# Moving the second low part of each weight load from VectorE to GpSimd

## The chip, the cores and the metric

The kernel runs on one core of a Trainium2 chip. The metric is device time in microseconds (us). A core has five engines that run side by side, each working through its own queue in order and waiting on semaphores: TensorE (PE in the profile; PEld are its weight loads), VectorE (DVE), ScalarE (ACT), GpSimd (POOL) and SyncE (SP), which here issues nearly all DMA transfers. VectorE, ScalarE and GpSimd work on SBUF, the on-chip memory of 128 partitions; TensorE writes its products to PSUM, from where VectorE or ScalarE take them.

## The reference

One layer of a hybrid network runs over 384 tokens: 128 of a context stream and 256 of a latent stream, with a model width of 2048.

```python
z = h @ w_in                                  # h: normalised, modulated input
zs = _token_shift(z[..., :N_SHIFTED], mu_prev, mu_next)
r, k, v, wd, ad = ...                         # slices of zs
w_lin = w0 + einsum(tanh(wd), w2);  a = sigmoid(a0 + einsum(ad, a2))
sa = S @ a_t                                  # scan, both directions, 32 heads of 64 x 64
S = S * w_t + outer(sa, b_t) + outer(v_t, k_t);  y = S @ r_t
y_a = (groupnorm(y) + bonus) * silu(g_a) @ w_out_a
y_b = (b_gate * conv3(c_gate * x_b) * silu(g_b)) @ w_out_b
merged = sigmoid(m_a) * y_a + sigmoid(m_b) * y_b
out = x + gate * (merged @ w_o)
```

All inputs are float32. The large matrices (w_in with 20,864 columns, w_out_a, w_out_b, w_o) make up most of the work.

## The kernel before, in words

A float32 product is made of three products of a rounded format: each operand x is split into a high part (a cast) and a low part (x minus the high part), and TensorE adds high x high, high x low and low x high (`mm3`, lines 80 to 83). For a weight, ScalarE casts the high part (`whi`, line 88) and VectorE subtracts to get the low part (`wlo`, line 89); both happen in `split`.

Dense work is a stream of column pairs (`Stream`). A pair is two blocks of 128 columns over 2048 rows, loaded in two halves of 1024 rows. A half is one call of `wload`: it takes a buffer `raw` (two in rotation, 1 MB each, filled by one DMA or by two when the columns are apart), and splits it in two parts of 512 rows, q = 0 and q = 1. `whi` and `wlo` each have three buffers. TensorE uses a part in 24 matmuls. There are 95 pairs: `rk` (r and k of a head pair), `gv` (gate and v), `ma`, `mb`, `bc`, `bx`, `bg`, `gb` (gates and convolution), `ob` and `oa` (the output projections of the branches). A `raw` buffer is free for its next load when both subtractions from it are done.

The recurrence runs in 16 blocks b of two heads. Block b goes through `prep_a` and `prep_k` (decays and keys), `prep_b` (triangular systems), `prep_c` (transposes) and `scan` (two chains of chunks in both directions), then `norm` and `finish`. The steps on which this document rests are these.

- `prep_b` multiplies `pr` and `bk` on TensorE (`pA`, line 703), VectorE masks the result into `A` (line 709), and the diagonal blocks go through DRAM into a tile `U` of 48 partitions: `ui<-A` (line 713) and `U<-ui` (line 719), both on SP. VectorE then runs sixty dependent operations on `U` and `ut` (lines 724 and 726), after which SP writes `uo<-U` (line 729) and reads it back, `A<-uo` (line 734). VectorE transposes two pieces (`x<-A`, line 737), which TensorE needs at the scan's start (`pH`, line 842).
- Meanwhile GpSimd scales `bk` (line 716), and the next block's `prep_a` multiplies low-rank weights (`pl`, line 627 through `mm3`), whose low part `lwl` VectorE makes in `split` too, and a sum of squares (`pn`) whose low part is `lo_sq` (line 605). v is shifted on VectorE (lines 422 and 424).
- In `scan`, TensorE's `pu` goes to the state `st` on VectorE (L831 at the first step, L833 later), the state to `po` on TensorE (line 804), that to `sav` on VectorE (L805), and so on. The next block's `prep_k` (L646, L647, L654, L659 to L661) shares VectorE's queue with it.
- GpSimd also clears a part of `A` (line 863) and takes a power in `norm` (line 929).

TensorE's queue is written out by hand: the generators yield numbers of dense steps to put between their own matmuls. The queues of the other engines are set by the framework's scheduler, from its own estimates and priorities, and it is run anew for every version of the program.

Of the kernel before, what the change touches and what calls it, by code (L numbers as in the profile page):

```python
# [9 lines left out]
F32 = mybir.dt.float32  # L10
F32R = mybir.dt.float32r
AF = mybir.ActivationFunctionType
ALU = mybir.AluOpType
AX = mybir.AxisListType

P = 128
# [40 lines left out]
def hybrid_step(ctx, tc, cst, x_prompt, x_sample, state_f, state_b, c, c_ctx, ada_w, ada_b, norm_g,  # L57
# [3 lines left out]
    V, S, G, TE = nc.vector, nc.scalar, nc.gpsimd, nc.tensor  # L61
# [6 lines left out]
    wp = ctx.enter_context(tc.tile_pool(name="wp", bufs=3))  # L68
# [13 lines left out]
        TE.matmul(out, wh, xl, start=False, stop=False)  # L82
        TE.matmul(out, wl, xh, start=False, stop=stop)  # L83

    def split(src, shape, th, tl, pool, nm, rows=P):
        hi = pool.tile(shape, F32R, tag=th, name=f"{th}_{nm}")
        lo = pool.tile(shape, F32R, tag=tl, name=f"{tl}_{nm}")
        S.copy(hi[0:rows], src)  # L88
        V.tensor_tensor(lo[0:rows], src, hi[0:rows].bitcast(F32), ALU.subtract)  # L89
        return hi, lo  # L90


# [3 lines left out]
    def wload(view, k0, cols, nm):  # L96

        w = P * len(cols)
        raw = wp.tile([P, 8, w], F32, tag="raw", name=f"raw_{nm}", bufs=2)
        if cols[-1] == cols[0] + P:  # L100
            nc.sync.dma_start(raw[:], view[:, k0:k0 + 8, cols[0]:cols[0] + 256])
        else:
            for i, c0 in enumerate(cols):
                nc.sync.dma_start(raw[:, :, i * P:(i + 1) * P], view[:, k0:k0 + 8, c0:c0 + P])
        res = [split(raw[:, 4 * q:4 * q + 4, :], [P, 4, w], "whi", "wlo", wp, f"{nm}_{q}") for q in range(2)]
        return res


# [2 lines left out]
    class Stream:  # L111
# [14 lines left out]
        def load(self, j):  # L126
            p, half = divmod(j, 2)
            self.extend(p)
            if j not in self.ready and p < len(self.pairs):
                tag, view, cols = self.pairs[p][:3]  # L130
                self.ready[j] = wload(view, 8 * half, cols, f"{tag}_{half}")
# [207 lines left out]
    def early_load(g):  # L339
        raw = wp.tile([P, 2, EW], F32, tag="raw", name=f"eraw_{g}", bufs=2)  # L340
        o = 0
        for c0, w in ecols:
            nc.sync.dma_start(raw[:, :, o:o + w], win[:, 2 * g:2 * g + 2, c0:c0 + w])
            o += w
        return split(raw[:], [P, 2, EW], f"ehi{g % 2}", f"elo{g % 2}", pp, f"{g}")
# [212 lines left out]
    for m in range(4):  # L558
# [10 lines left out]
        src = t[0:96, ::-1] if m % 2 else t[0:96, :]  # L569
# [38 lines left out]
    def prep_a(b, o):  # L608
# [9 lines left out]
        for m in range(4):  # L618
            if m % 2 == 0:
                lraw = sp.tile([96, 2, P], F32, tag="lraw", name=f"lraw_{b}_{m}")  # L620
                nc.sync.dma_start(lraw[:], (w2, a2)[m // 2][0][:, :, bs].rearrange("d r n -> r d n"))
                with tc.issue_after(box["kn"]) if m == 0 and "kn" in box else ExitStack():
                    lwh, lwl = split(lraw[:], [96, 2, P], "lwh", "lwl", sp, f"{b}_{m}", rows=96)
                yield 2
            pl = bank(f"pl_{b}_{m}")
            pl = flat(pl[:, 0:3, :])
            mm3(pl, lwh[:, m % 2, :], lwl[:, m % 2, :], l_hi[:, m, :], l_lo[:, m, :], True, True)
            t = tmp(f"sig_{b}_{m}")
            S.activation(t[:], pl, AF.Sigmoid, bias=pcol((W0, W0 + 16, A0, A0 + 16)[m] + b))
            sig.append(t)  # L630
            yield 2
# [329 lines left out]
    for b in range(NB):  # L961
# [17 lines left out]
        w = WINDOW + (FIRST if b == 0 else LAST if b == NB - 1 else 0)  # L979
# [108 lines left out]
    for nq in range(3):  # L1088
# [8 lines left out]
        for q in range(4):  # L1097
            raw = wp.tile([P, 4, 512], F32, tag="raw", name=f"raw_wo{nq}_{q}", bufs=2)
            nc.sync.dma_start(raw[:], wov[:, 4 * q:4 * q + 4, ns])
            for e in range(2):  # L1100
                hi, lo = split(raw[:, 2 * e:2 * e + 2, :], [P, 2, 512], "whi", "wlo", wp, f"wo{nq}_{q}_{e}")
# [11 lines left out]
    for half in range(2):  # L1113
        c0 = 1536 + 256 * half
        wt = []
        for q2 in range(2):
            raw = wp.tile([P, 8, 256], F32, tag="raw", name=f"raw_wl{half}_{q2}", bufs=2)
# [4 lines left out]
        for s in range(3):  # L1122
# [5 lines left out]
            for k in range(KC):  # L1128
                hi, lo = wt[k // 4]
# [3 lines left out]
            if half == 1:  # L1133
                f = rsf[:, s, :]
# [37 lines left out]
```

## Time and profile before

| | |
|---|---|
| runs of the kernel before | 2236.75, 2238.54, 2238.73 us, median 2238.54 |
| profiled execution | 2234.36 us, span 2232.6 us, granted TensorE clock 0.998 |
| TensorE, matmuls | 2173.1 us busy, 97% of the span |
| VectorE | 1553.3 us busy, 70% |
| ScalarE | 1013.5 us busy, 45% |
| GpSimd | 115.7 us busy, 5% |
| HBM | 305.80 MB read, 26.21 MB written |

A row of a timeline has start, duration, engine, line, operation, tile written and tiles read, shapes and count; in brackets the idle time before it and what ended it. Merged rows (x2, x3) give the time from the first start to the last end. "PEq" or "SPq" marks an engine's sequencer; a DMA's issue is shown there, not its transfer. A row of waits has the total in us, the number of times, and the longest. A row of a group has its busy time, the mean of one in ns, and the idle time before.

### The profile page before, as it was taken

The numbers are of one execution on the slowest core, as the hardware profiler recorded it, in microseconds if no ns is written. First come the engines' busy times: TensorE is split into PE (matmuls) and PEld (weight loads), VectorE is DVE, ScalarE is ACT, GpSimd is POOL, SyncE is SP. The second block draws the span as 40 slices with busy tenths as digits, with TensorE's granted clock in tenths as the row PEclk, the third lists the DMA queues.
The fourth block names the chain that finished last, engine by engine and source line by source line (L and its number), as shares of the span: only waits on it lengthen the run. The fifth ranks groups of instructions, "written<-read, shape, count | busy, mean of one in ns | idle before, by whom it ended". The sixth has DMA issues, their size and how long they took to land.

```text
span 2232.6 us, 40518 instructions
## 1 busy us (share of the span) xinstructions
PE 2173.1 (97%) x16020; PEld 2062.7 (92%) x16020; DVE 1553.3 (70%) x3240; ACT 1013.5 (45%) x1784; POOL 115.7 (5%) x113
## 2 busy tenths in 40 slices
PE   5999999999999999999999999999999999999998
PEld 3589999999999999999999999999999999998988
DVE  3259567787878878777878787887777785444354
ACT  4245435454545454444445454546454633333333
POOL 2000000000000000000000000000000000000000
PEclk9999999999999999999999999999999999999999
DMA  9974454444343435343444434344445464886633
GB/s 338 346 211 128 131 141 116 116 117 118 108 132 107 130 100 131 106 130 100 121 108 127 112 107 133 107 122 126 124 118 139 144 196 143 294 281 233 220 132 113
DMA packets 426574, 335.25 MB, mean 150 GB/s; under 512 B 82496, under 2 KB 408720, under 8 KB 425488
## 3 DMA queue, kind: packets, MB, share of 16 engines
q1 hardware_dynamic: 424896, 330.91, 50.2%
q8 instruction: 126, 2.06, 0.4%
q10 hardware_dynamic: 432, 1.57, 0.2%
q14 instruction: 64, 0.52, 0.1%
q0 software_dynamic: 1056, 0.19, 0.1%
HBM read 305.80 MB, written 26.21 MB: 149 GB/s over the span
## 4 chain that ended last, share of the span: by engine, by line
PE 74%; DVE 12%; DMA 6%; ACT 4%; issue 2%; SPq 1%; POOL 0%; POOLq 0%; DVEq 0%; ACTq 0%
DMA raw_adah<-in_ada_w_dram 4%; PE d_rk L81 3%; PE d_rk L82 3%; PE d_rk L83 3%; PE d_gv L81 3%; PE d_gv L82 3%; PE d_gv L83 3%; PE d_oa L81 2%; PE pA L703 2%; PE d_oa L83 2%; PE d_oa L82 2%; PE d_mb L81 2%; PE d_mb L83 2%; PE d_mb L82 2%; PE d_bc L81 2%
## 5 line engine op out<-in xcount | busy, mean ns | idle before, releaser
L724 DVE TENSOR_TENSOR ut<-U 48x30 f32<-48x30 f32 (+14 forms) x480 | 154.8, 323 | 18.3 <-DMA U<-ui 5.5
L81 PE MATMUL d_rk<-h_hi,whi_rk 128*128 128x384 f32 x480 | 161.7, 337 | 0.6 <-ACT lst L554 0.6
L726 DVE TENSOR_TENSOR U<-U,ut 48x30 f32<-48x30 f32 (+14 forms) x480 | 154.5, 322 | 11.1
L81 PE MATMUL d_gv<-h_hi,whi_gv 128*128 128x384 f32 x480 | 160.6, 335 | 0.0
L82 PE MATMUL d_rk<-h_lo,whi_rk 128*128 128x384 f32 x480 | 160.5, 334 | 0.0
L83 PE MATMUL d_rk<-h_hi,wlo_rk 128*128 128x384 f32 x480 | 160.4, 334 | 0.0
L83 PE MATMUL d_gv<-h_hi,wlo_gv 128*128 128x384 f32 x480 | 160.4, 334 | 0.0
L82 PE MATMUL d_gv<-h_lo,whi_gv 128*128 128x384 f32 x480 | 160.4, 334 | 0.0
L88 ACT CAST whi_gv<-raw_gv 128x1024 fp32r<-128x1024 f32 (+1 forms) x64 | 64.0, 999 | 139.6 <-PE d_rk L82 100.0
L88 ACT CAST whi_rk<-raw_rk 128x1024 fp32r<-128x1024 f32 x60 | 63.0, 1054 | 110.8 <-PE d_rk L82 34.7
L89 DVE TENSOR_TENSOR wlo_rk<-raw_rk,whi_rk 128x1024 fp32r<-128x1024 f32 x60 | 72.9, 1218 | 45.3 <-ACT whi_rk L88 35.6
L81 PE MATMUL d_bc<-h_hi,whi_bc 128*128 128x384 f32 x256 | 92.2, 360 | 0.0
L81 PE MATMUL d_gb<-h_hi,whi_gb 128*128 128x384 f32 x256 | 92.2, 360 | 0.0
L81 PE MATMUL d_bg<-h_hi,whi_bg 128*128 128x384 f32 x256 | 92.2, 360 | 0.0
L81 PE MATMUL d_bx<-h_hi,whi_bx 128*128 128x384 f32 x256 | 92.1, 360 | 0.0
L81 PE MATMUL d_ma<-h_hi,whi_ma 128*128 128x384 f32 x256 | 91.6, 358 | 0.0
L81 PEld LDWEIGHTS d_rk<-h_hi,whi_rk 128*128 128x128 f32 x480 | 90.1, 188 | 0.9 <-ACT lst L554 0.9
L81 PE MATMUL d_mb<-h_hi,whi_mb 128*128 128x384 f32 x256 | 90.4, 353 | 0.0
L81 PEld LDWEIGHTS d_gv<-h_hi,whi_gv 128*128 128x128 f32 x480 | 90.1, 188 | 0.2
L81 PE MATMUL d_ob<-ybh,whi_ob 128*128 128x384 f32 x256 | 88.4, 345 | 2.0 <-DVE smb L521 1.0
L82 PEld LDWEIGHTS d_rk<-h_lo,whi_rk 128*128 128x128 f32 x480 | 90.2, 188 | 0.0
L82 PEld LDWEIGHTS d_gv<-h_lo,whi_gv 128*128 128x128 f32 x480 | 90.1, 188 | 0.0
(315 smaller groups left out, 6548.4 us busy)
## 6 DMA issues: line engine op xcount, KB each, us to landing
raw_adah<-in_ada_w_dram SPq DMA_DIRECT2D x64, 512.0 KB, 8.7
raw_rk<-in_w_in_dram SPq DMA_DIRECT2D x60, 512.0 KB, 5.3
raw_gv<-in_w_in_dram SPq DMA_DIRECT2D x60, 512.0 KB, 4.9
raw_ma<-in_w_in_dram SPq DMA_DIRECT2D x16, 1024.0 KB, 5.6
raw_mb<-in_w_in_dram SPq DMA_DIRECT2D x16, 1024.0 KB, 5.6
raw_bc<-in_w_in_dram SPq DMA_DIRECT2D x16, 1024.0 KB, 5.5
raw_bx<-in_w_in_dram SPq DMA_DIRECT2D x16, 1024.0 KB, 5.4
raw_bg<-in_w_in_dram SPq DMA_DIRECT2D x16, 1024.0 KB, 5.5
```

The lines of the kernel that those rows point to most:

```text
L81: TE.matmul(out, wh, xh, start=start, stop=False)
L82: TE.matmul(out, wh, xl, start=False, stop=False)
L83: TE.matmul(out, wl, xh, start=False, stop=stop)
L88: S.copy(hi[0:rows], src)
L89: V.tensor_tensor(lo[0:rows], src, hi[0:rows].bitcast(F32), ALU.subtract)
L703: TE.matmul(pas[h, n // 4 * 4][:, n % 4, :], bk[hss[h], n, :], pr[hss[h], n, :], start=True, stop=True)
L724: V.tensor_tensor(tv, U[:, 0:s, s:s + 1].broadcast_to([48, s, w]), U[:, s:s + 1, s + 1:].broadcast_to([48, s, w]), ALU.mult)
L726: V.tensor_tensor(U[:, 0:s, s + 1:], U[:, 0:s, s + 1:], tv, ALU.add)
```

## The change

The helper `split` gets a parameter for the engine that subtracts, and `wload` passes VectorE for the first part of a half and GpSimd for the second. All other users of `split` keep VectorE. The file becomes one line longer, so from there on the lines of the changed kernel are one higher.

```diff
-    def split(src, shape, th, tl, pool, nm, rows=P):
+    def split(src, shape, th, tl, pool, nm, rows=P, eng=V):
         hi = pool.tile(shape, F32R, tag=th, name=f"{th}_{nm}")
         lo = pool.tile(shape, F32R, tag=tl, name=f"{tl}_{nm}")
         S.copy(hi[0:rows], src)
-        V.tensor_tensor(lo[0:rows], src, hi[0:rows].bitcast(F32), ALU.subtract)
+        eng.tensor_tensor(lo[0:rows], src, hi[0:rows].bitcast(F32), ALU.subtract)
         return hi, lo
...
-        res = [split(raw[:, 4 * q:4 * q + 4, :], [P, 4, w], "whi", "wlo", wp, f"{nm}_{q}") for q in range(2)]
+        res = [split(raw[:, 4 * q:4 * q + 4, :], [P, 4, w], "whi", "wlo", wp, f"{nm}_{q}", eng=(V, G)[q])
+               for q in range(2)]
```

TensorE's queue is the same before and after. GpSimd's gains 190 subtractions, in the order of the loads, between its own scalings, clearings and powers. The scheduler also moves other operations on VectorE, ScalarE and SP. Three places follow, all in block 5.

VectorE at the start of the scan, before: after the last piece of `A` (L878) come the reciprocals of the next block's `prep_k`, its first decay scan (L654), a low part, then the first state (L831) and the second chain's (L833).

```order
L878 COPY A_7358<-pX_8060 32x6x32 x2
L646 RECIPROCAL kn_7955<-kn_7955 128x128 x3
L654 SCALAR_TENSOR_TENSOR L_0_8105<-cs,sig_0_7896 128x384
L89 TENSOR_TENSOR wlo_bc_0_1_8046<-raw_bc_0_8039,whi_bc_0_1_8045 128x1024
L831 COPY st_1144<-pu_0_0_8143 64x2x64 x2
L647 SCALAR_TENSOR_TENSOR kn_7955<-kk_7860,kn_7955 128x384
L659 TENSOR_SCALAR kd_0_8109<-sig_2_7932,par,omka 128x384
L833 TENSOR_TENSOR st_1146<-pu_1_0_8159,ls_1_0_8031 64x2x64 x2
L660 TENSOR_TENSOR kd_0_8109<-k_7722,kd_0_8109 128x384
L661 TENSOR_TENSOR sig_2_7932<-kn_7955,sig_2_7932 128x384
```

VectorE at the same place, changed (lines one higher: L655 is L654, L832 is L831):

```order
L879 COPY A_7358<-pX_8060 32x6x32 x2
L647 RECIPROCAL kn_7955<-kn_7955 128x128 x3
L655 SCALAR_TENSOR_TENSOR L_0_8105<-cs,sig_0_7896 128x384
L648 SCALAR_TENSOR_TENSOR kn_7955<-kk_7860,kn_7955 128x384
L660 TENSOR_SCALAR kd_0_8109<-sig_2_7932,par,omka 128x384
L655 SCALAR_TENSOR_TENSOR L_1_8113<-cs,sig_1_7908 128x384
L832 COPY st_1144<-pu_0_0_8143 64x2x64 x2
L661 TENSOR_TENSOR kd_0_8109<-k_7722,kd_0_8109 128x384
L662 TENSOR_TENSOR sig_2_7932<-kn_7955,sig_2_7932 128x384
L834 TENSOR_TENSOR st_1146<-pu_1_0_8159,ls_1_0_8031 64x2x64 x2
```

The low part is gone from here. Three operations of `prep_k` (L648, L660, the second L655) now stand ahead of the state L832, and two more ahead of L834.

VectorE at the end of the chain of U, before:

```order
L724 TENSOR_TENSOR ut_7454<-U_7452 48x30
L726 TENSOR_TENSOR U_7452<-U_7452,ut_7454 48x30
L89 TENSOR_TENSOR wlo_gb_0_1_7798<-raw_gb_0_7791,whi_gb_0_1_7797 128x1024
L440 TENSOR_TENSOR ga_7837<-ga_7837,d_gv_0_7730 128x384
L89 TENSOR_TENSOR wlo_gb_1_0_7879<-raw_gb_1_7876,whi_gb_1_0_7878 128x1024
L422 SCALAR_TENSOR_TENSOR v_7852<-zs_7853,par,v_7852 128x127
L422 SCALAR_TENSOR_TENSOR v_7852<-zs_7853,par,v_7852 128x255
L424 SCALAR_TENSOR_TENSOR v_7852<-zs_7853,par,v_7852 128x127
L424 SCALAR_TENSOR_TENSOR v_7852<-zs_7853,par,v_7852 128x255
L605 TENSOR_TENSOR lo_sq_7865<-sq_7862,sqh_7864 128x384
L89 TENSOR_TENSOR lwl_2_7919<-lraw_2_7916,lwh_2_7918 96x256
L737 STREAM_TRANSPOSE x_5_7517<-A_7358 32x384 x2
```

VectorE at the same place, changed (L738 is L737, L606 is L605):

```order
L725 TENSOR_TENSOR ut_7454<-U_7452 48x30
L727 TENSOR_TENSOR U_7452<-U_7452,ut_7454 48x30
L441 TENSOR_TENSOR ga_7837<-ga_7837,d_gv_0_7730 128x384
L738 STREAM_TRANSPOSE x_5_7517<-A_7358 32x384
L89 TENSOR_TENSOR wlo_gb_1_0_7879<-raw_gb_1_7876,whi_gb_1_0_7878 128x1024
L738 STREAM_TRANSPOSE x_5_7517<-A_7358 32x384
L423 SCALAR_TENSOR_TENSOR v_7852<-zs_7853,par,v_7852 128x127
L423 SCALAR_TENSOR_TENSOR v_7852<-zs_7853,par,v_7852 128x255
L425 SCALAR_TENSOR_TENSOR v_7852<-zs_7853,par,v_7852 128x127
L425 SCALAR_TENSOR_TENSOR v_7852<-zs_7853,par,v_7852 128x255
L606 TENSOR_TENSOR lo_sq_7865<-sq_7862,sqh_7864 128x384
L89 TENSOR_TENSOR lwl_2_7919<-lraw_2_7916,lwh_2_7918 96x256
```

The two transpositions of `x`, which read `A` back from DRAM, stood behind lo_sq and lwl; now they stand ahead of them, and ahead of the shifts of v. So it is in blocks 3, 5, 7, 9, 11, 13 and 14; in the even blocks from 2 to 12 they stay behind lwl. Between the chain's first and last operation three low parts stand on VectorE (gv, gv, gb; six before), and in GpSimd's queue four more follow in the same stretch (rk, gv, gv, gb).

SP around the same chain, before:

```order
L713 DMA ui_7356<-A_7358 32x12x32 x4
L104 DMA raw_gv_0_7655<-in_w_in_dram 128x8x128
L719 DMA U_7452<-ui_7356 48x1024
L104 DMA raw_gv_0_7655<-in_w_in_dram 128x8x128
L104 DMA raw_gv_1_7732<-in_w_in_dram 128x8x128 x2
L101 DMA raw_gb_0_7791<-in_w_in_dram 128x8x256
L101 DMA raw_gb_1_7876<-in_w_in_dram 128x8x256
L729 DMA uo_7357<-U_7452 48x1024
L101 DMA raw_bc_0_8039<-in_w_in_dram 128x8x256
L734 DMA A_7358<-uo_7357 32x12x32 x4
L621 DMA lraw_0_9024<-in_w_dram 96x2x128
```

SP, changed (L720 is L719, L735 is L734):

```order
L714 DMA ui_7356<-A_7358 32x12x32 x4
L104 DMA raw_gv_0_7655<-in_w_in_dram 128x8x128 x2
L720 DMA U_7452<-ui_7356 48x1024
L104 DMA raw_gv_1_7732<-in_w_in_dram 128x8x128 x2
L101 DMA raw_gb_0_7791<-in_w_in_dram 128x8x256
L101 DMA raw_gb_1_7876<-in_w_in_dram 128x8x256
L730 DMA uo_7357<-U_7452 48x1024
L735 DMA A_7358<-uo_7357 32x12x32 x4
L101 DMA raw_bc_0_8039<-in_w_in_dram 128x8x256
L622 DMA lraw_0_9024<-in_w_dram 96x2x128
```

Both transfers of the first gv half now stand ahead of U's; before, U's stood between them. The transfer of raw_bc, which stood between uo and A, now follows A. In even blocks a load that stood ahead of uo now stands between uo and A, and lraw follows A.

## The prediction

> **What bounds the kernel now.** I read the page's shares first, then TensorE's list of waits, then the timelines of blocks 5 and 6 (blocks are counted from 0; these begin near 730 and 835 us). The first two:
>
> ```profile
> span 2232.6 us, 40518 instructions
> PE 2173.1 (97%) x16020; PEld 2062.7 (92%) x16020; DVE 1553.3 (70%) x3240; ACT 1013.5 (45%) x1784; POOL 115.7 (5%) x113
> ...
> PE pada L292 <- DMA raw_adah<-in_ada_w_dram: 22.4, 16, 9.4
> PE po L804 <- DVE st L833: 7.6, 9, 1.6
> ```
>
> TensorE is busy 97% of the span, and 22.4 us of its idle time belong to the prologue's loads, which the change leaves alone. VectorE is at 70%, so relieving it is worth only the waits that it causes; the largest is 7.6 us in the scan. A gain is therefore capped near 8 us. A loss is not capped: TensorE's order is fixed by hand, so whatever arrives late stops everything behind it. The question is how late VectorE's chain becomes when GpSimd works beside it.
>
> **The price of a moved part.** 95 column pairs are loaded in two halves, 190 loads; the second low part of each moves, 186 of 1024 columns and 4 of 512.
>
> ```profile
> L89 DVE TENSOR_TENSOR wlo_rk<-raw_rk,whi_rk 128x1024 fp32r<-128x1024 f32 x60 | 72.9, 1218 | 45.3 <-ACT whi_rk L88 35.6
> L716 POOL TENSOR_TENSOR bk<-bk,ep 128x768 f32<-128x768 f32 x32 | 49.3, 1541 | 155.6 <-PE pA L703 140.9 <-DMA ui<-A 10.1 <-issue 4.6
> ```
>
> VectorE gives up 186 x 1.22 + 4 x about 0.7 = 230 us. No GpSimd subtraction of this size is in the trace; the nearest row is L716, 768 elements in 1.5 us, one operand a repeated column. In proportion, 1024 elements take 2.0 us. Below, 1.5 us, if that row is mostly fixed cost; above, 3.0 us, if the second full stream adds half again. I take 2.0 us: GpSimd gains about 380 us of work, still idle four fifths of the time. The busy times alone would say "free". What they leave out stands here (GpSimd's row, then VectorE's beside it):
>
> ```profile
> 304.59 1.49 POOL L716 TENSOR_TENSOR bk<-bk,ep 128x768 f32<-128x768 f32 x1 [5.21 <-PE pA L703]
> ...
> 304.15 0.55 DVE L939 TENSOR_TENSOR ya<-ya,bon 128x384 f32<-128x384 f32 x1
> 304.62 0.68 DVE L709 TENSOR_TENSOR A<-pA,cs 128x512 f32<-128x512 f32 x1
> 305.22 1.27 DVE L940 TENSOR_TENSOR ya<-ya,ga 128x384 f32<-128x384 f32 x1
> ```
>
> L939 and L940 are the same operation on the same shape. L939 ran before GpSimd's and took 0.55 us; L940 began inside it and took 1.27, ending at 306.49. Its own 0.55 us thus began at 305.94, about GpSimd's end (306.08). L709, with one input in PSUM, ran beside GpSimd undisturbed. So a VectorE operation with two SBUF inputs stands still while GpSimd works on SBUF. The Trainium skill (Perfetto Trace Analysis, GPSIMD Engine Instruction) warns that a GpSimd span is unreliable; here VectorE's release agrees with it within 0.15 us. A moved part hence spares VectorE 1.2 us of its own and may hold it for 2.0.
>
> The Trainium skill (GPSIMD Engine Reference, 3.1 Elementwise side-by-side) gives 4497 ns for 2048 elements against VectorE's 2293; half of that, an estimate, is 2.25 us, and by it the sum below would come to about 120 us instead of 99.5. VectorE's half, 1.15 us, is near the 1.22 measured here; GpSimd's no row of this trace shows.
>
> **Place 1, the scan's start (blocks 1 to 14).** VectorE, then ScalarE, then TensorE in block 5:
>
> ```profile
> 794.76 2.55 DVE L646 RECIPROCAL kn<-kn 128x128 f32<-128x128 f32 x3
> 797.25 0.88 DVE L654 TENSOR_TENSOR_SCAN L<-cs,sig 128x384 f32<-128x384 f32 x1
> 798.06 1.19 DVE L89 TENSOR_TENSOR wlo_bc<-raw_bc,whi_bc 128x1024 fp32r<-128x1024 f32 x1
> 799.27 0.59 DVE L831 COPY st<-pu 64x128 f32<-64x128 f32 x2
> 799.90 0.56 DVE L647 SCALAR_TENSOR_TENSOR kn<-kk,kn 128x384 f32<-128x384 f32 x1
> 800.37 0.48 DVE L659 TENSOR_SCALAR kd<-sig,par,omka 128x384 f32<-128x384 f32 x1
> ...
> 796.32 1.05 ACT L88 CAST whi_bc<-raw_bc 128x1024 fp32r<-128x1024 f32 x1 [0.27 <-PE d_gb L82]
> ...
> 800.60 0.34 PE L83 MATMUL d_gb<-h_hi,wlo_gb 128*128 128x384 f32 x1
> 800.78 0.27 PE L804 MATMUL po<-st,pr 128*128 128x128 f32 x1
> ```
>
> L831 ends at 799.86 and TensorE's po, which reads it, starts at 800.78: 0.9 us to spare. The low part there moves away, but in the new queue L647, L659 and the second L654 stand ahead of L831 in its stead. From 798.06, counting start to start: 0.47 + 0.5 + 0.81 + L831's 0.59, end 800.4, still in time. But the cast ends at 797.37, so GpSimd asks at once and gets its turn either when L654 ends (holding until 800.1, before L647) or after L647 (holding until 800.6; L659, with one tensor input, can run meanwhile, the second L654 can't). L831 then ends at 802.5 or 802.0. TensorE waits 1.7 or 1.2; I take 1.5. Fourteen blocks: **21 us**. Behind L831 the two chains' next steps (L660, L661, L833) are shifted alike and add nothing.
>
> **Place 2, the chain of U and what is queued behind it.** SP, VectorE, the low parts inside the chain (746 to 775.2), and block 1's queue, where two loads precede U:
>
> ```profile
> 740.12 0.39 SPq L104 DMA_DIRECT2D raw_gv<-in_w_in_dram  x1
> 740.69 0.44 SPq L719 DMA_DIRECT2D U<-ui  x1
> ...
> 746.08 0.18 DVE L724 TENSOR_TENSOR ut<-U 48x30 f32<-48x30 f32 x1 [0.30 <-DMA U<-ui]
> 775.12 0.20 DVE L726 TENSOR_TENSOR U<-U,ut 48x30 f32<-48x30 f32 x1
> ...
> L89 DVE TENSOR_TENSOR wlo_gv<-raw_gv,whi_gv 128x1024 fp32r<-128x1024 f32 x4 | 4.8, 1208 | 0.0
> L89 DVE TENSOR_TENSOR wlo_rk<-raw_rk,whi_rk 128x1024 fp32r<-128x1024 f32 x1 | 1.2, 1210 | 0.0
> L89 DVE TENSOR_TENSOR wlo_gb<-raw_gb,whi_gb 128x1024 fp32r<-128x1024 f32 x1 | 1.2, 1208 | 0.0
> ...
> 312.28 1.02 SPq L104 DMA_DIRECT2D raw_rk<-in_w_in_dram  x2
> 313.48 1.02 SPq L719 DMA_DIRECT2D U<-ui  x1
> ...
> 319.49 0.18 DVE L724 TENSOR_TENSOR ut<-U 48x30 f32<-48x30 f32 x1 [1.75 <-DMA U<-ui]
> ```
>
> Start of U: raw_gv waits on SP for the rk load's second low part, 0.8 us later on GpSimd (2.0 against 1.2); now both raw_gv issues stand before U's, 0.5 us more (740.12 to 740.69 for one); and U lands behind two loads, as in block 1, in 6.0 us instead of 5.4: 0.6. Together 1.9 us. Inside: six low parts before, three now (-3 x 1.21 = -3.6), but four of GpSimd's fall into the chain, whose sixty operations all have two SBUF inputs: +4 x 2.0. The chain ends 1.9 + 4.4 = 6.3 us later. In block 6 the queue of before has seven inside: 5.1.
>
> What waits for it: odd blocks (block 5), then even ones (block 6).
>
> ```profile
> 775.36 0.34 SPq L729 DMA_DIRECT2D uo<-U  x1
> 778.02 1.88 SPq L734 DMA_DIRECT2D A<-uo  x4
> ...
> 779.18 0.74 DVE L422 SCALAR_TENSOR_TENSOR v<-zs,par,v 128x127 f32<-128x127 f32 x2
> 780.96 0.41 DVE L89 TENSOR_TENSOR lwl<-lraw,lwh 96x256 fp32r<-96x256 f32 x1
> 782.78 1.14 DVE L737 STREAM_TRANSPOSE x<-A 32x384 f32<-32x384 f32 x2 [1.40 <-DMA A<-uo]
> ...
> 782.55 0.34 PE L83 MATMUL pl<-l_hi,lwl 96*128 96x384 f32 x1
> ...
> 888.38 1.86 SPq L734 DMA_DIRECT2D A<-uo  x4
> ...
> 882.51 0.21 DVE L726 TENSOR_TENSOR U<-U,ut 48x30 f32<-48x30 f32 x1
> 886.30 0.41 DVE L89 TENSOR_TENSOR lwl<-lraw,lwh 96x256 fp32r<-96x256 f32 x1
> 890.34 0.57 DVE L737 STREAM_TRANSPOSE x<-A 32x384 f32<-32x384 f32 x1 [0.47 <-DMA A<-uo]
> ...
> 887.89 0.34 PE L83 MATMUL pl<-l_hi,lwl 96*128 96x384 f32 x1
> ```
>
> Before, lwl (the low-rank weight's low part) is ready at 781.37 and TensorE needs it at 782.55: 1.2 us to spare. In the new queue of odd blocks both L737 stand ahead of it, and they wait for U's round trip through DRAM. Chain end 775.32 + 6.3 = 781.6; to A's issue 2.7 (775.36 to 778.02); to the first L737 2.0 (888.38 to 890.34, where no load stands between): 786.3. Then L737, one low part, L737: 0.57 + 1.21 + 0.57; the shifts and lo_sq 1.8 (779.18 to 780.96); lwl 0.4: 790.9. TensorE waits 790.9 - 782.55 = 8.3 us, of which 2.0 come from the queue's order alone. In even blocks lwl still precedes L737 and ends 4.0 us after the chain (886.71 - 882.72), against 5.2 to TensorE's need: 5.1 - 1.2 = 3.9. Seven blocks (3, 5, 7, 9, 11, 13, 14) x 8.3 = **58**, six (2 to 12) x 3.9 = **23.4**. Blocks 0, 1 and 15 have other fills; I count nothing. L842, which needs L737, comes 5 us behind and is shifted by as much.
>
> **The sum.** 58 + 23.4 + 21 = 102.4, less 3 of the 7.6 us of L833's waits: +99.5. On the profiled execution's 2234.4 us that is 2334 us; its time is 4 us (0.2%) under the median of the runs, 2238.5, so the same sum there would be 2338. With 1.5 us for GpSimd's part: odd 5.8, even 1.4, place 1 1.0, +60, 2294. With 3.0: 13.3, 8.9, 2.5, +178, 2412. The rest is covered: a low part is used 24 products (0.18 us each, 800.60 to 800.78) at a time out of three buffers, so it may come some 7 us after its cast.
>
> **The rivals.**
> - *Faster.* Low parts no longer stand in VectorE's queue ahead of L833 and po never waits: 7.6 us less, 2227. For it: the wait is real. Against: only where GpSimd finds VectorE idle, and 305.22 shows the opposite. It decides if GpSimd's part blocks VectorE for under 1.2 us. 6%.
> - *Hidden.* The blocking is an accident of that row, both run side by side: U's chain shortens by 3.6 and starts 1.9 later, odd blocks wait 8.3 - 8.0 = 0.3, place 1 nothing: +2, 2236. Against: the two equal operations. 8%.
> - *Half.* GpSimd gets through mostly while VectorE handles PSUM operands or waits, so that half of its time in U's chain costs nothing: odd 4.3, even 0, place 1 1.0: +41, 2275. For it: L709 was free. Against: the sixty operations have no such gap. 15%.
> - *Late weights.* GpSimd's part takes over 7 us, so L83 itself waits; at 9 us, 2 us for each of 190 loads, 2610. Against: 1.5 us at 768 elements. 5%.
>
> **How the numbers follow.** The forecast has 66%, its own range 2294 to 2412. Slower: 66 + 15 + 5 = 86%; no change, within 0.2% (about what a measurement here can tell), 8%; faster 6%. For 8 in 10 the range goes from 2250, which takes in the half case, to 2400.
>
> **What would show it.** Right: L89 on GpSimd near 2.0 us; U's chain 33 to 34 us instead of 29.2 in odd blocks; TensorE's list led by pl L83 <- DVE lwl, 8 us each, then po <- DVE st, 1 to 2 us each. Wrong: VectorE's operations keep their length beside GpSimd's; or U's chain grows and pl does not wait; or L83 waits for wlo.

## The result, and the profile after

The changed kernel is slower: 2452.14 us (median of four runs, 2445.99 to 2457.36) against 2237.68 before (median of four), a ratio of 1.0957 (95% interval 1.093 to 1.0984). That is 214 us more, where 99.5 were forecast. The direction held; the time lies outside the range.

The profiled execution, from the page:

```profile
span 2449.2 us, 40664 instructions
PE 2241.1 (92%) x16020; PEld 2109.7 (86%) x16020; DVE 1592.0 (65%) x3050; ACT 997.3 (41%) x1772; POOL 606.2 (25%) x303
```

and from the list of spans and granted clocks by core:

```profile
core 0: 2449.2 us, clock 0.972
```

The span grew by 216.6 us (2449.2 - 2232.6). It splits in two: TensorE's idle time grew by 148.6 (208.1 against 59.5), and its busy time by 68.0 (2241.1 against 2173.1), although it runs the same 16020 products. Most of the second part has a name in the last row: the granted clock was 0.998 before and is 0.972 now. An estimate: TensorE was busy for 114.2 us in stretches at half clock (3.4 before), and there a product of 128x384 starts every 0.32 us instead of every 0.174, so about 50 of the 68 us are the slower clock. The other 18 were not traced; TensorE paused more often (106 pauses of over 0.15 us, 51 before), and the products on both sides of a pause count in full (0.34 and 0.44 us around the wait for wlo_gv shown below; without a pause one starts every 0.17). VectorE gave up 190 subtractions and is busier than before (1592 against 1553 us).

TensorE's list of waits (total, times, longest) says where the idle time is:

```profile
PE d_gv L83 <- DVE wlo_gv L89: 47.5, 23, 3.2
PE pl L83 <- DVE lwl L89: 28.9, 7, 5.9
PE py L937 <- DVE ytok L931: 26.0, 15, 3.1
PE po L805 <- DVE st L832: 25.8, 14, 1.9
...
PE po L805 <- DVE st L834: 10.4, 6, 2.1
```

The low parts named here are VectorE's own, not GpSimd's. U's chain and what is queued behind it (place 2) cost 47.5 + 28.9 us, the scan's start (place 1) 25.8 + 10.4 where L833 alone cost 7.6 before. The 26 us of py, at the norm, were in no term of the forecast.

How VectorE loses the time, inside U's chain of block 5 (GpSimd, then VectorE):

```profile
829.37 2.85 POOL L89 TENSOR_TENSOR wlo_gv<-raw_gv,whi_gv 128x1024 fp32r<-128x1024 f32 x1 [6.56 <-ACT whi_gv L88]
...
829.30 0.39 DVE L727 TENSOR_TENSOR U<-U,ut 48x234 f32<-48x234 f32 x1
829.62 0.34 DVE L423 SCALAR_TENSOR_TENSOR r<-zs,par,r 128x127 f32<-128x127 f32 x1
829.88 2.58 DVE L725 TENSOR_TENSOR ut<-U 48x228 f32<-48x228 f32 x1
```

GpSimd's row begins at 829.37 and ends at 832.22. Its shortest part took 2.34 us, so it seems to have waited until L423 was through (829.96) before it worked. L725, which took 0.38 us on this shape before (L724), starts at 829.88 and ends at 832.46, just after it. The two engines take turns, each for a whole instruction. The chain that took 29.2 us before ran from 811.20 to 846.00 here, 34.8 us.

VectorE's own low part in the middle of that chain (ScalarE's cast, VectorE's subtraction, TensorE):

```profile
823.32 1.05 ACT L88 CAST whi_gv<-raw_gv 128x1024 fp32r<-128x1024 f32 x1 [0.99 <-POOL wlo_gv L89]
834.35 1.21 DVE L89 TENSOR_TENSOR wlo_gv<-raw_gv,whi_gv 128x1024 fp32r<-128x1024 f32 x1
835.61 0.44 PE L83 MATMUL d_gv<-h_hi,wlo_gv 128*128 128x384 f32 x1 [2.73 <-DVE wlo_gv L89]
```

It is ready 11.2 us after its cast; before, VectorE's low parts of gv in this chain were ready 2.0 to 3.0 us after theirs.

The scan's start of block 4, GpSimd, VectorE and TensorE:

```profile
748.09 3.49 POOL L89 TENSOR_TENSOR wlo_bx<-raw_bx,whi_bx 128x1024 fp32r<-128x1024 f32 x1 [9.03 <-ACT whi_bx L88]
...
749.12 2.67 DVE L660 TENSOR_SCALAR kd<-sig,par,omka 128x384 f32<-128x384 f32 x1
...
752.67 0.59 DVE L832 COPY st<-pu 64x128 f32<-64x128 f32 x2
...
754.97 0.48 DVE L660 TENSOR_SCALAR kd<-sig,par,omka 128x384 f32<-128x384 f32 x1
...
753.41 0.68 PE L805 MATMUL po<-st,pr 128*128 128x128 f32 x4 [1.88 <-DVE st L832]
```

L660 reads one tensor and took 2.67 us beside GpSimd, 0.48 alone; L832 behind it is late, and po waits 1.88.

The norm of block 4, GpSimd, VectorE and TensorE:

```profile
786.35 1.32 POOL L930 TENSOR_TENSOR rs<-var,nhalf 128x6 f32<-128x6 f32 x1 [10.11 <-DVE var L928]
787.64 2.34 POOL L89 TENSOR_TENSOR wlo_bg<-raw_bg,whi_bg 128x1024 fp32r<-128x1024 f32 x1
...
787.71 2.69 DVE L931 TENSOR_TENSOR ytok<-ytok,rs 128x384 f32<-128x384 f32 x1 [1.44 <-POOL rs L930]
1974.00 0.56 DVE L931 TENSOR_TENSOR ytok<-ytok,rs 128x384 f32<-128x384 f32 x1 [1.43 <-POOL rs L930]
...
790.54 0.52 PE L937 MATMUL py<-cs,ytok 128*128 128x128 f32 x3 [3.10 <-DVE ytok L931]
```

GpSimd finishes the power that VectorE waits for, and its next instruction, a low part, runs first: L931 needs 2.69 us, and py is late. This happens in 15 blocks. In the remaining one, block 14 (the row at 1974.00), no low part follows the power at once, and L931 takes 0.56 us.

The half clock, in stretches of 3.41 us (length, TensorE's busy time with its instructions, granted clock, DMA share, GB/s), first around the wait for wlo_gv at 832.9 to 835.6:

```profile
832.70:836.11 3.41, 0.68 (x5) 1.00 0.00 0
836.11:839.52 3.41, 3.41 (x12) 0.50 0.77 234
839.52:842.94 3.42, 3.42 (x21) 1.00 0.24 78
```

In a stretch in which TensorE was busy for 0.68 of 3.41 us nothing happens yet; in the next one it gets half the clock and does 12 products instead of 21, and then the clock is back. Every such stretch of the trace begins a whole multiple of 3.413 us after every other: there is a fixed grid. TensorE had 2 of them in the trace before (in the first 40 us and at the very end), and 32 entries now, nearly all of one or two windows (the last is TensorE's end).

### The profile page after: what moved, and what is told of

The parts are those of the page before. It is cut to its first block, busy times and chain, and to the rows that moved or that the text cites. A ratio compares the mean times of both kernels' runs of the same rounds, so it can differ in the third digit from the quotient of the medians.

```text
span 2449.2 us, 40664 instructions
## 1 busy us (share of the span) xinstructions
PE 2241.1 (92%) x16020; PEld 2109.7 (86%) x16020; DVE 1592.0 (65%) x3050; ACT 997.3 (41%) x1772; POOL 606.2 (25%) x303
## 4 chain that ended last, share of the span: by engine, by line
PE 28%; DVE 14%; issue 4%; DMA 3%; ACT 2%; POOL 1%; SPq 0%; DVEq 0%; POOLq 0%; ACTq 0%
DVE ut L725 3%; DVE U L727 3%; PE d_oa L81 2%; PE d_oa L83 2%; PE d_oa L82 2%; PE acc L81 1%; PE acc L83 1%; PE acc L82 1%; DMA yst_a<-ya_d 1%; DMA U<-ui 1%; PE d_ob L81 1%; PE d_ob L82 1%; PE d_ob L83 1%; PE pA L704 1%; DVE kd L660 1%
## 5 line engine op out<-in xcount | busy, mean ns | idle before, releaser
L725 DVE TENSOR_TENSOR ut<-U 48x30 f32<-48x30 f32 (+14 forms) x480 | 228.8, 477 | 48.6 <-DMA U<-ui 35.6
L83 PE MATMUL d_gv<-h_hi,wlo_gv 128*128 128x384 f32 x480 | 169.2, 353 | 48.8 <-DVE wlo_gv L89 47.5
L727 DVE TENSOR_TENSOR U<-U,ut 48x30 f32<-48x30 f32 (+14 forms) x480 | 202.0, 421 | 13.3
L81 PE MATMUL d_gv<-h_hi,whi_gv 128*128 128x384 f32 x480 | 166.3, 346 | 0.0
L82 PE MATMUL d_gv<-h_lo,whi_gv 128*128 128x384 f32 x480 | 166.2, 346 | 0.0
L83 PEld LDWEIGHTS d_gv<-h_hi,wlo_gv 128*128 128x128 f32 x480 | 94.7, 197 | 56.8 <-DVE wlo_gv L89 55.1
L89 POOL TENSOR_TENSOR wlo_gv<-raw_gv,whi_gv 128x1024 fp32r<-128x1024 f32 (+1 forms) x32 | 83.9, 2623 | 204.7 <-ACT whi_gv L88 195.2
L89 POOL TENSOR_TENSOR wlo_rk<-raw_rk,whi_rk 128x1024 fp32r<-128x1024 f32 x30 | 75.9, 2530 | 166.6 <-ACT whi_rk L88 149.6
L83 PE MATMUL d_bg<-h_hi,wlo_bg 128*128 128x384 f32 x256 | 89.5, 350 | 3.7 <-DVE wlo_bg L89 3.7
L83 PE MATMUL d_bx<-h_hi,wlo_bx 128*128 128x384 f32 x256 | 88.9, 347 | 4.1 <-DVE wlo_bx L89 4.1
```

What stands on the lines that cost most here:

```text
L81: TE.matmul(out, wh, xh, start=start, stop=False)
L89: eng.tensor_tensor(lo[0:rows], src, hi[0:rows].bitcast(F32), ALU.subtract)
L725: V.tensor_tensor(tv, U[:, 0:s, s:s + 1].broadcast_to([48, s, w]), U[:, s:s + 1, s + 1:].broadcast_to([48, s, w]), ALU.mult)
L727: V.tensor_tensor(U[:, 0:s, s + 1:], U[:, 0:s, s + 1:], tv, ALU.add)
```

## The experiments

Theory A is that of the prediction: GpSimd's reading of SBUF makes VectorE stand still. Rival B: the new order of VectorE's queue does it. Rival C: any GpSimd work in those places does it.

**GpSimd's work alone.** The kernel before, with one GpSimd instruction more per load:

```diff
         res = [split(raw[:, 4 * q:4 * q + 4, :], ...) for q in range(2)]
+        gj = wp.tile([P, 4, 2 * P], mybir.dt.bfloat16, tag="gj", ...)
+        G.tensor_tensor(gj[:, :, 0:w], raw[:, 4:8, :], res[1][0][:].bitcast(F32), ALU.subtract)
```

> The kernel before, with one GpSimd instruction more for each load: the same subtraction of the second part, written to a scratch tile in bfloat16 that nobody reads; VectorE still makes both low parts, and the queues of TensorE, VectorE, ScalarE and SP keep the order of before. Theory A (GpSimd's subtraction holds VectorE, whoever computes the low part): slower by 150 to 300 us, that is 2390 to 2540, with U's chain 8 to 10 us longer (four GpSimd parts of 2.4 us) and TensorE waiting for po, py, lwl or wlo. Rival B (the new order of the queues is what costs; GpSimd's work beside VectorE is nearly free): within 10 us of before, 2228 to 2248.

Measured: 2515.16 us against 2237.58, ratio 1.1249 (1.123 to 1.1268), 278 us more. From its list of waits:

```profile
PE d_gv L83 <- DVE wlo_gv L89: 49.0, 28, 2.7
PE py L936 <- DVE ytok L930: 34.0, 15, 3.4
PE po L804 <- DVE st L833: 30.3, 24, 2.4
```

Large waits for wlo_gv, ytok and st again, with the queues of the kernel before. Theory A holds, and the new order isn't needed for a loss. The wait for lwl is the exception: 10.7 us in all here, and about 0.5 us in each odd block from 3 to 11, where the change waits 5.1 to 5.9. In the change both L737 stand ahead of lwl, here they stand behind it. That this run is slower than the change itself probably comes from VectorE's own subtractions, which it keeps all; no run separates that.

**Writing instead of reading.** Here the GpSimd instruction is replaced:

```diff
+        gj = wp.tile([P, 2, 2 * P], F32, tag="gj", ...)
+        G.tensor_copy(gj[:, 0, 0:1], res[1][0][:, 0, 0:1].bitcast(F32))
+        for _ in range(5): G.memset(gj[:], 0.0)
```

> As the run with the scratch subtraction, but GpSimd only reads one column of the high part (so that it starts at the same moment) and then clears a scratch tile of 512 columns five times: about as long, but it writes SBUF and reads nearly nothing. Queue orders as before on the other engines. Theory A in its narrow form (only GpSimd work that reads SBUF holds VectorE): within 10 us of before, 2228 to 2248, and VectorE's operations keep their length beside the clearings. Rival C (any GpSimd work in those places, or its semaphores, delays VectorE and the loads): slower by over 100 us, like the scratch subtraction.

Measured: 2245.47 us, ratio 1.0038 (1.0023 to 1.0053). Within the 10 us, though not zero: 8 us more. GpSimd was busier than in any other run (784 us), so neither its busy time nor its semaphores are the cause; rival C falls. What is left may come from the copy of one column. It shows the other side of the turn-taking (GpSimd, then VectorE):

```profile
558.23 3.00 POOL L105 COPY gj_gv<-whi_gv 128x1 f32<-128x1 f32 x1 [5.20 <-ACT whi_gv L88]
...
559.69 1.21 DVE L89 TENSOR_TENSOR wlo_gv<-raw_gv,whi_gv 128x1024 fp32r<-128x1024 f32 x1
560.83 0.36 DVE L726 TENSOR_TENSOR U<-U,ut 48x210 f32<-48x210 f32 x1
561.22 0.36 DVE L724 TENSOR_TENSOR ut<-U 48x198 f32<-48x198 f32 x1
```

One column takes GpSimd 0.18 us when it is alone. Here it took 3.00: VectorE's operations from 558.02 on each begin before the one ahead has ended, and only between 561.19 and 561.22 is there a gap.

**Fewer loads, by tag.** Two complements of each other:

```diff
-                     ..., eng=(V, G)[q])
+                     ..., eng=(V, G)[q] if nm[:2] in ("rk", "gv") else V)    # rk and gv
+                     ..., eng=V if nm[:2] in ("rk", "gv") else (V, G)[q])    # the rest
```

> The changed kernel, but GpSimd takes the second low part only of the rk and gv loads (60 of 190); those are three of the four GpSimd parts inside U's chain, and none lies at the scan's start or at the norm. Theory A: the waits for lwl and wlo_gv stay at about three quarters of the 76 us of the changed kernel (57) and their stretches at half clock with them (20), the waits for po (36) and py (26) go back to 8 and 0: 2238 + 57 + 20 = 2315, between 2290 and 2350. If the losses came from all 190 loads evenly, 60/190 of 214 us: 2306 with po and py waiting as well; the list of waits tells them apart.

> The complement: GpSimd takes the second low part of all loads but rk and gv (130 of 190). Theory A: the waits for po (36, before 8) and py (26) stay, with the dense ones for wlo_bx, wlo_bg and others (10), of the U place one GpSimd part of four (19), and half-clock stretches of 25 to 30 us: 2238 + 28 + 26 + 10 + 19 + 28 = 2349, between 2320 and 2370. With the rk and gv run it should add up to the whole, 214 us, within 40 us. If the places interact (a wait in one gives slack in the next), the two add up to more than 214.

Measured: 2353.69 (ratio 1.0525, 1.0502 to 1.0548) and 2327.9 (1.0409, 1.0393 to 1.0424), that is 116 and 90 us. Their lists, rk and gv first:

```profile
PE d_gv L83 <- DVE wlo_gv L89: 44.7, 23, 3.0
PE pl L83 <- DVE lwl L89: 27.8, 15, 4.0
```

```profile
PE po L805 <- DVE st L832: 26.3, 14, 2.4
PE py L937 <- DVE ytok L931: 26.2, 15, 3.1
```

The places belong to the loads as expected, and 116 + 90 = 206 of 214 us: they add up. But rk and gv alone cost nearly the whole of place 2 (72.5 of 76.4 us), not three quarters of it, so the first run came out 3.7 us above its range. In the second, U's chain still ends later (31.5 us from the first operation to the last in block 5), and TensorE waits for nothing there that it did not wait for before (lwl 1.7 us, wlo_gv none): one GpSimd part in the chain is covered by the slack ahead of lwl.

**The changed order without the reads.** GpSimd clears the low part where it subtracted it; VectorE's queue is nearly that of the change:

```diff
-        eng.tensor_tensor(lo[0:rows], src, hi[0:rows].bitcast(F32), ALU.subtract)
+        if eng is V:
+            V.tensor_tensor(lo[0:rows], src, hi[0:rows].bitcast(F32), ALU.subtract)
+        else:
+            G.tensor_copy(lo[:, 0, 0:1], hi[:, 0, 0:1].bitcast(F32))
+            for _ in range(2): G.memset(lo[:].bitcast(F32), 0.0)
```

> The changed kernel, but where GpSimd subtracted it now reads one column of the high part and then clears the low part twice (about 2.2 us of GpSimd's time, nearly no reads); the low part of the second part of every load is left out of the computation. VectorE is relieved of the same 190 subtractions; its queue is that of the changed kernel but for 57 of 2743 rows. Theory A (the reads hold VectorE): the loss is gone, 2230 to 2248, with po, py, lwl and wlo_gv waiting no more than before (about 10 us in all) and the mean clock back at 0.995 or above. Rival B (the new order of VectorE's queue costs a good part): above 2290 with the same waits.

Measured: 2228.57 us against 2237.73, ratio 0.996 (0.9946 to 0.9974): 9 us faster than before, just under the lower end of the expectation. Its page, and from its list of waits the one left in the scan:

```profile
PE 2175.3 (98%) x16020; PEld 2064.0 (93%) x16020; DVE 1341.5 (60%) x3050; ACT 1001.1 (45%) x1772; POOL 551.3 (25%) x683
```

```profile
PE po L810 <- DVE st L839: 3.5, 7, 0.7
```

Rival B falls: the changed order alone costs nothing that the relief of VectorE doesn't outweigh, and lwl is waited for 1.6 us in all. Together with the first run this suggests that the long waits for lwl need both, GpSimd's reads and the new order; no run changes the order of L737 alone. The run also says what the relief is worth if nothing holds VectorE: 9 us together with the new order, where the forecast put the cap near 8.

**One input instead of two.** As the first experiment, with `G.tensor_copy(gj[:, :, 0:w], res[1][0][:].bitcast(F32))`.

> The kernel before, with a GpSimd copy of the high part into a bfloat16 scratch tile after each load's second part (one input instead of the two of the scratch subtraction); the queues of the other engines keep the order of before. If any long read of SBUF by GpSimd holds VectorE, the loss goes with the copy's length: 277 us at the 2.9 us of the scratch subtraction, so about 90 to 180 us for a copy of 1.0 to 1.8 us (2330 to 2420). If only two inputs on GpSimd's side collide, it is within 15 us of before, like the clearings (2245).

Measured: 2281.09 us, ratio 1.0201 (1.0183 to 1.0219), 43 us. GpSimd and VectorE in U's chain:

```profile
763.12 1.04 POOL L105 CAST gj_rk<-whi_rk 128x1024 bf16<-128x1024 f32 x1 [8.03 <-ACT whi_rk L88]
...
762.85 0.31 DVE L726 TENSOR_TENSOR U<-U,ut 48x150 f32<-48x150 f32 x1
763.19 1.15 DVE L724 TENSOR_TENSOR ut<-U 48x168 f32<-48x168 f32 x1
```

A read with one input holds VectorE too: 1.15 us in place of 0.33, to GpSimd's end. The expected proportion was wrong: half the length (1.23 against 2.51 us in the median) costs a sixth of the time. Probably a hold of 1 us mostly fits into slack that 2.4 us overrun; no run tests that.

**The half clock.** Four runs. In the first two TensorE gets work that nobody reads where it waits; the second has the filling ahead of pl alone:

```diff
                     po = bank(f"po_{b}_{ch}_{i}")
+                    for _ in range(10 if ch == 0 and i == 1 else 0):        # first run only
+                        TE.matmul(po[:, 2, :], bt[:, f0, :], sav[:, f0, :], start=True, stop=True)
...
             pl = flat(pl[:, 0:3, :])
+            for _ in range(24 if m == 2 and b in (4, 6, 8, 10, 12) else 0): # both runs
+                TE.matmul(pl, bones_r[:], h_hi[0], start=True, stop=True)
```

> The changed kernel with more work for TensorE where it waits: ten 128x128 products into an unused part of po's bank ahead of the first po of each block, and 24 products of 128x384 into pl's bank ahead of the product that waits for lwl in blocks 3, 5, 7, 9 and 11 (all overwritten or never read). Theory (a window of 3.41 us in which TensorE is busy for less than about 46% is followed by one at half clock): the waits turn into busy time, of the 30 stretches at half clock the 6 behind L832's waits and the 10 windows of the five lwl waits go, worth 10.5 and 10.9 us of slow products: 2452 - 21 = 2431, between 2422 and 2440, mean clock 0.98 or above. Rival (the half clock costs nothing of its own, or the gate goes by something else than busy time): unchanged or slower, 2445 to 2470.

> The changed kernel with only the second filling: 24 products of 128x384 (0.175 us each, 4.2 us, 120 in all) into pl's bank ahead of the product that waits for lwl, in blocks 3, 5, 7, 9 and 11; all are overwritten. VectorE's, GpSimd's and SP's queues keep the order of the changed kernel row for row, so nothing but TensorE's busy share during those five waits changes. Theory (a 3.41 us window with TensorE busy under about 46% is followed by one at half clock): the waits for lwl fall from 5.1 to 5.9 us to 1.0 to 1.7, the ten windows at half clock there disappear, and with them 10.9 us of slow products: 2452 - 11 = 2441, between 2435 and 2447, though TensorE does 21 us more work. Rival (the half clock costs nothing, or is not set by the busy share): 2448 to 2458, the windows still there.

Measured: the first 2466.7 us (ratio 1.1026, 1.101 to 1.1042), a miss. The po waits were filled, but the scheduler took po to be later and put five more of VectorE's operations ahead of sav, so that TensorE waited 28.7 us for sav instead. The run tells nothing of the clock. The second 2444.4 us (1.0931, 1.0915 to 1.0948), inside its range, 7.7 us under the changed kernel with 21 us more of TensorE's work. Block 3, TensorE, in this run, and then the same product in the changed kernel:

```profile
605.64 4.39 PE L629 MATMUL pl<-h_hi,bones_r 128*128 128x384 f32 x24
...
611.65 0.44 PE L83 MATMUL pl<-l_hi,lwl 96*128 96x384 f32 x1 [1.27 <-DVE lwl L89]
611.93 0.34 PE L81 MATMUL d_bx<-h_hi,whi_bx 128*128 128x384 f32 x1
612.11 0.34 PE L82 MATMUL d_bx<-h_lo,whi_bx 128*128 128x384 f32 x1
```

```profile
611.98 0.69 PE L83 MATMUL pl<-l_hi,lwl 96*128 96x384 f32 x1 [5.14 <-DVE lwl L89]
612.46 0.52 PE L81 MATMUL d_bx<-h_hi,whi_bx 128*128 128x384 f32 x1
612.78 0.52 PE L82 MATMUL d_bx<-h_lo,whi_bx 128*128 128x384 f32 x1
```

lwl comes at nearly the same moment in both; what follows it runs at 0.18 us a product with the filling and at 0.32 without. All five places show it. The time alone proves less: the intervals of the two ratios, 1.0915 to 1.0948 and 1.093 to 1.0984, touch.

So the clock was tested once more on the kernel before, where nothing else is changed: a pause of TensorE made once a block, with GpSimd work that only writes (gw is a tile of 128x512; n is 2 or 5):

```diff
         py = bank(f"py2_{b}")
+        TE.matmul(py[:, 3, :], gw[:, 0:P], gw[:, 0:P], start=True, stop=True)
+        for _ in range(n): G.memset(gw[:], 0.0)
+        TE.matmul(py[:, 3, :], gw[:, 0:P], gw[:, 0:P], start=True, stop=True)
```

> The kernel before (VectorE makes all low parts), with a pause of TensorE made on purpose once in each of the 16 blocks, ahead of py2 at the end of the scan: a small product reads a scratch tile, GpSimd then clears the tile twice (0.53 us each, no reads), a second small product waits for that. The pause should be 1.2 to 1.5 us. Theory (half clock only after a 3.41 us window with TensorE busy under about 46%, that is idle for more than 1.84 us): none of the pauses can do that, mean clock 0.996 or above, time 2238 + 16 x 1.4, less up to 5 us of other waits that get slack: 2255 to 2262. If any pause of TensorE halves the clock: 16 windows of 1.7 us more, 2280 or above.

> The same with five clearings, a pause of 2.8 to 3.1 us. Against the grid of windows of 3.41 us a pause of 3.0 us leaves more than 1.84 us of idle time in one window at 80% of its possible places, so about 13 of 16 pauses should be followed by a window at half clock, each costing 1.5 to 1.7 us: theory 2238 + 16 x 3.0 + 13 x 1.6 - 5 = 2302, between 2290 and 2312, mean clock near 0.990. Rival (half clock needs a whole window without work, 3.41 us, so that no pause of 3 us does it): mean clock 0.996 or above, 2238 + 48 - 5 = 2281, between 2275 and 2287.

Measured: 2269.08 us (ratio 1.0138, 1.0121 to 1.0155), with the clock at 0.998, and 2327.51 us (1.0398, 1.0383 to 1.0414), with the clock at 0.980. The pauses by the list of waits, two clearings and five:

```profile
PE py L896 <- POOL gw L895: 20.9, 16, 1.6
```

```profile
PE py L896 <- POOL gw L895: 48.9, 16, 3.3
```

Sixteen pauses of 1.3 us cost their own length and 0.7 us each for the small products (7 us above the range, which had left those out); none was followed by half clock. Of sixteen pauses of 3.0 us, 15 were. The 28 us by which the longer pauses differ account for about half of the 58 us between the two runs; TensorE's busy time, 32.8 us larger on the same work, accounts for the rest. A pause of less than a whole window is enough. The second run is 15 us above its range because its sum had left out the small products too (12 us in the other run), and because seven of the 15 were followed by two windows at half clock, not one, as here:

```profile
740.00:743.41 3.41, 0.97 (x7) 0.99 1.01 280
743.41:746.83 3.42, 2.82 (x42) 0.50 0.12 28
746.83:750.24 3.41, 3.41 (x23) 0.51 0.12 17
```

The middle window is busy for 82%, and the clock stays at half. Over all fourteen profiled runs (from the clock's records and TensorE's rows of products, on the grid of 3.413 us, from 195 us to 20 us before TensorE's end): of 156 windows at full clock that were busy for less than 45%, 153 were followed by half clock; of 55 between 45 and 49%, 33; of 8231 above that, 3. Of 229 windows at half clock, the 34 busy for less than 80% were all followed by another, the 184 above 88% by none, of the 11 between, 6. The Trainium skill (TensorE: Matmul & The Clock Gate, What's actually happening) gives the same window of 3413 ns and half clock "after ≥1 idle window (~3.4µs)"; here the window need not be idle as a whole, 55% of it suffices, and the measurement decides.

**The norm.** In the changed kernel, the product that GpSimd holds up is done by GpSimd:

```diff
-        V.tensor_tensor(y6, y6, rs[:].unsqueeze(2).broadcast_to([P, 6, C]), ALU.mult)
+        G.tensor_tensor(y6, y6, rs[:].unsqueeze(2).broadcast_to([P, 6, C]), ALU.mult)
```

> The changed kernel, but the product of ytok and rs, which VectorE does while GpSimd's next subtraction holds it (2.7 us in place of 0.5), is done by GpSimd itself right behind rs; the other queues are those of the changed kernel (9 rows of VectorE's and GpSimd's that move). Theory A: the py waits of 26 us fall to below 8 and the few half-clock stretches behind them go: 2452 - 20 to 30 = 2422 to 2434. Rival (py waits for something else of the norm, for instance the chain ahead of rs): py's waits stay, 2445 to 2460.

Measured: 2434.17 us (ratio 1.087, 1.0843 to 1.0896), 0.2 us above the upper end of the range. py's waits fell from 26.0 to 2.8 us (now for GpSimd's product), and the cause is shown; 9 us of it came back as waits for lwl (37.9 us, before 28.9).

**A faster kernel?** The clearing run suggested that relieving VectorE pays where nothing holds it. ScalarE took one of its operations in the kernel before:

```diff
-            V.tensor_scalar(kd[:], aa[:], pcol(KA + b), omka[:, b:b + 1], ALU.mult, ALU.add)
+            S.activation(kd[:], aa[:], AF.Identity, scale=pcol(KA + b), bias=omka[:, b:b + 1])
```

> The kernel before, with the first of the two operations on kd in the keys' preparation (L659, a scaling by two values per partition, 0.48 us, 32 times) done by ScalarE instead of VectorE. It follows from the run without GpSimd's reads, which was 9 us faster than before: relieving VectorE at the scan's start is worth something when nothing holds it. Theory: the po waits behind L833 (7.6 us) fall by half or more: 2238 - 4 to 7 = 2231 to 2234. Rival (ScalarE's queue makes kd later than VectorE did, or the order of the queues eats it): 2236 to 2245.

Measured: 2239.32 us, ratio 1.0005 (0.9996 to 1.0014), no change. The po waits fell from 7.6 to 1.9 us, and other waits (3.2 us for a gate on VectorE, 2.4 for a cast on ScalarE, 1.5 for another) came in their place. No version that makes every low part was found that beats the kernel before.

## Why the prediction was wrong

*What bounds it, and which way.* Right: TensorE's fixed order, a gain capped near 8 us (9 measured without GpSimd's reads, in a run that leaves the second low part of each load out), a loss not capped. The reading of the two equal operations, L939 and L940, as a standstill of VectorE was right, and the two runs with scratch instructions show it: 278 us for a read, 8 for as long a write. The Trainium skill (SBUF — State Buffer, Who interferes with whom) has this rule: a VectorE instruction with two SBUF inputs contends with a GpSimd one that reads SBUF, not with one that only writes; both runs agree.

*The price, "I take 2.0 us".* Too small. The 186 GpSimd parts of 128x1024 took 2.39 us in the median (2.34 at least). That is nearer to 2.25, the estimate by the page of the Trainium skill that the prediction names (GPSIMD Engine Reference, 3.1 Elementwise side-by-side), than to the 2.0 in proportion to the row of 768 elements with its repeated column. It lies between the bounds, and the sum's own slope, 178 us at 3.0 against 99.5 at 2.0, gives 130 us at 2.39.

*Place 2.* "The chain ends 6.3 us later": its length grew from 29.2 to 34.8 us (33 to 34 expected), and it started about 2 us later (from pA's first product, 16.5 us before and 20.2 now, of which 1.5 are pA's own slow clock); 1.9 was forecast. The sum, 81.4 us, was near the measured 76.4 (wlo_gv 47.5, pl 28.9), but partly by luck, since the errors cancel. In the odd blocks from 3 to 11 the two waits make 46 us where 41.5 were counted, in the even blocks from 2 to 12 they make 20.3 where 23.4 were, in blocks 13 and 14 6.5 in place of 16.6 (only three of GpSimd's parts fall into the chain there, it takes 31.8 us, and pl does not wait), and in the first blocks 3.5 in place of nothing. What was wrong is who waits: I followed the chain to its end, to lwl, and counted VectorE's low parts inside it as work, not as something awaited. The step that failed is "The rest is covered", by which a low part may come some 7 us after its cast: the wlo_gv in the middle of the chain is held up with the rest, comes 11.2 us after its cast in block 5, and TensorE needs it first. Its wait of up to 3.2 us then shortens the one for lwl: in block 5, 0.5 + 2.73 + 5.87 = 9.1 us in all, 8.3 forecast; in the even blocks pl does not wait at all.

*Place 1.* 14 waits of 1.84 us, 25.8 us, where 14 x 1.5 = 21 was forecast: near, with one sentence wrong. The 1.5 was a middle value between two turns. GpSimd's turn came after L647, for which 1.2 us was worked out, but "L659, with one tensor input, can run meanwhile" is wrong: in all 14 blocks it stood still (2.66 against 0.48 us), and its own 0.48 us came on top. The 3 us taken off for L833 were the other way, 2.8 more.

*The missing terms.* Two make most of the miss. First the norm, 26.0 us: the neighbours were in sight (GpSimd's power, with the low part next in its queue), but I priced only the places that the scheduler had reordered. The turn-taking happens wherever GpSimd's part meets VectorE, moved or not. Second TensorE's slower clock: its busy time grew by 68.0 us, about 50 of them at half clock, and the sum put this at nothing without a reason. I multiplied waits by one, as if a pause cost its own length. In a window at half clock 11 products fit in place of 20 (3.41 us at 0.32 and at 0.174 each), so a pause of over 1.85 us inside a window cost up to about 1.6 us more, and one followed by two such windows up to 3.1.

In sum, for the profiled executions: forecast 99.5, measured 216.6. Idle time, forecast 99.5, grew by 148.6 (place 2 76.4 less 1.7 before; place 1 28.6; norm 26.0; the remaining 19 in small waits, 11 of them for other low parts and 6 for one operand of the output projection); busy time, forecast 0, grew by 68.0. Of the rivals, none came true: *half* was the wrong way (the sixty operations do have gaps of 0.03 us, and GpSimd uses them to get in, not VectorE to get on), *late weights* is 1.3 us in all.

## What to carry to other kernels

An engine whose reads of SBUF make a busy one stand still is not free, however idle it is: price a moved operation by its whole length on every dependent chain that it can meet, and look at each place where the two are neighbours, not only where the order changed. Where the matmul engine waits, count the wait and then look at the window: a pause that takes more than about 55% of one window of 3.41 us also halves the clock of the next. A test with a scratch instruction that leaves all other queues as they are costs little and separates "the engine is busy" from "the data is read" from "the order is new".

## What the runs showed of the hardware that was not expected

- TensorE's clock is gated on a fixed grid of 3.413 us. A window with TensorE busy for under 45% is followed by one at half clock (153 of 156; from 45 to 49% 33 of 55), and half clock ends only after a window that is busy for more than about 80 to 88%. Pauses of 1.3 us never did it (0 of 16); a pause of 1.85 us did when it fell into one window:

```profile
392.38:395.80 3.42, 1.57 (x11) 1.28 (x10) 3.33 (x7) 1.09 (x4) 0.61 (x1) 1.00 0.44 113
395.80:399.21 3.41, 3.41 (x14) 3.41 (x13) 3.33 (x9) 3.19 (x8) 0.00 (x0) 0.50 0.56 195
```

- VectorE's operation with one SBUF tensor and two values per partition (L660) is held by GpSimd like those with two inputs, 14 times of 14.
- The holding works both ways. A GpSimd copy of one column (0.18 us alone) took up to 6.2 us beside VectorE operations that overlap each other without a gap.
